# A two-layer diffusion backbone on one core: scratch tiles of their own in the merge, the last six feed-forward blocks by token groups, and five products ahead of layer 1's second norm

## The chip, the cores and the metric

The kernel runs on one core of a Trainium2 chip. The metric is the device time of one execution in microseconds (us); the median of several runs counts. The core has five engines, each of which works through its own queue in order: TensorE (PE in the profile; its weight loads are listed apart as PEld), VectorE (DVE), ScalarE (ACT), GpSimd (POOL) and SyncE (SP), which here only issues DMAs. Engines wait for each other by semaphores. Matmuls read SBUF and write PSUM.

## The reference

A diffusion backbone of two layers with D = 1024, over 512 latent tokens and 256 context tokens, 768 together. Cut to what matters:

```python
for l in range(2):
    mod = silu(c) @ w_mod[l] + b_mod[l]          # and mod_c from c_ctx, for the context tokens
    sh1, sc1, g1, sh2, sc2, g2 = split(mod, 6)
    h = rms_norm(x, norm1[l]) * (1 + sc1) + sh1
    na_q, na_k, na_v, gq, gk, gv, ga, gb = split(h @ w_in[l])
    ya = neighbourhood_attention(na_q, na_k, na_v)      # 8 heads, window 8 x 16, plus context
    yb = grouped_query_attention(gq, gk, gv)            # 8 query heads, 2 key heads
    merged = sigmoid(ga) * (ya @ w_pa[l]) + sigmoid(gb) * (yb @ w_pb[l])
    x = x + g1 * (merged @ w_o[l])
    h2 = rms_norm(x, norm2[l]) * (1 + sc2) + sh2
    a, u = split(h2 @ w_ffn_in[l], 2)                   # 2816 columns each
    x = x + g2 * ((silu(a) * u) @ w_ffn_out[l])
return rms_norm(x, final_norm)
```

The context tokens go through the same steps in layer 0; in layer 1 only the latent tokens are carried past the projections.

## The kernel before

**Tiles.** Activations are stored with the 1024 features in 8 tiles of 128 partitions (index k or j) and tokens along the free dimension. A float32 product is made of three reduced-precision ones: both operands are split into a high part and what is left of it (the low part), and TensorE does high by high, high by low and low by high for each of the 8 feature blocks. So a product of one 128-row block of weights with a span of tokens is 24 matmuls, of 512, 384 or 256 columns. `weight()` (L353) loads a block of weights into the ring `wr` (4 tiles), has ScalarE copy the high part into the ring `wh` (3 tiles, L357) and GpSimd, or VectorE where `eng` says so, subtract it into `wl` (3 tiles, L359). `halves()` (L381) does the same for an activation: ScalarE the tile `hi`, GpSimd the tile `lo`. All loads go through SP's one queue in the order they are issued in.

**Order.** The program is written engine by engine by a scheduler that simulates the program's timeline and so sets the order on each queue, except where the code holds TensorE's order by hand (`manual_schedule`): in the attention, and at the start of each layer's feed-forward, where `part` or `whole` products are listed in a fixed order and the second norm is put in between by due times (`NORM`, in us of TensorE's work: first the sum over squares `st`, then the broadcast `rb`).

**Merge** (`merge`, L1390 and following). Two branches, `gb` with yb and then `ga` with ya. For each of 8 blocks j: a gate product `pj` (its result t, a tile `qt`), the projection `pp`, and the sum into `mb` or into `mh` and `ml`. In layer 0 the modulation of the later parts (28 columns blocks, n from 16 to 43) is done beside it: `mod_one` (L434) loads 128 rows of `wmodT` and does two products with a sum on VectorE, one for the latent row of conditions (L441) and one for the context's (L439), whose full-size output is thrown away into a tile `junk`. `junk` and the scratch of `conditions` (L419) are taken from the ring `wh`. `MODS` says how many of these are done at each j. What is left of the 28 is done in layer 0's output projection, one per j.

**Layer 0's output projection** (`out_proj`) goes over two halves of 384 tokens, 8 blocks of `wo` each; per block a residual on VectorE, a square on ScalarE and its sum `acc` on VectorE.

**Layer 0's feed-forward** (`ffn`). Blocks f of 128 hidden columns, 22 in all; the first two are plain products, the other 20 are done as `quad`, a scheme of seven products of half size on each side for two by two blocks, with scratch tiles `tt` (`TEMPS` of them). The output product takes blocks by chunks of 4, woven in between the quads; the last chunk is what is left (blocks 20 and 21) and is done for one token group after the other, (0, 512) and (512, 768), with residual, square and `acc`. After each group `following` stores x and does the next layer's first norm for it.

**Norm.** `rstd` (L473 to L497): `st` matmuls over `acc`, VectorE adds the epsilon (`rs`, L493), GpSimd takes the power, `rb` matmuls spread it over partitions. `modulate` then does, per feature block, `u` on VectorE (L526), `h` on ScalarE (L527) and `hl` on VectorE (L528).

**Layer change.** Layer 1's first products are for `gk`, `gv` and `gq` 0, on the 512 latent tokens first and on the context after.

**Layer 1's second norm.** In layer 1 the output projection goes over two groups of 256 tokens; the second group's norm is what `late` puts into the start of `ffn_plain`, whose products for the first group (`pf`) run ahead of it. `ffn_plain` takes blocks f in four chunks and gives `qt` 5 tiles.

Functions that the change touches:

## Time and profile before

| | us |
|---|---|
| runs | 2028.03, 2028.92, 2032.21 |
| median | 2028.92 |
| profiled execution: time | 2031.42 |
| profiled execution: span | 2029.6 |
| PE busy | 1954.4 (96%) |
| DVE busy | 1373.0 (68%) |
| ACT busy | 884.9 (44%) |
| POOL busy | 532.4 (26%) |

The span is cut into 40 slices in the page; in tenths of a slice, and with the granted clock of TensorE in tenths of full speed:

```profile
PE   7999999989999999999999979999999989999998
...
PEclk7899999989999999999999989999999989999999
```

A slice is 50.7 us. The slices with a 7 or an 8 are the prologue, layer 0's merge (from about 430), the layer change (1177 to 1222), layer 1's second norm (1641 to 1666) and the end. Attention of layer 0 lies before 430, its output projection at 580 to 650, its feed-forward from there to 1177; layer 1's attention and merge run to about 1600, its feed-forward from 1650 to 2010. TensorE's share is an average; what a change is worth is read in the stretch it changes.

### The profile page before, as it was taken

The page shows a single profiled execution, that of the slowest core. Times are in us where ns is not written, and L with a number is a line of the kernel's source. Part 1 is how long each engine was busy: PE and PEld are TensorE (multiplying, and loading weights), DVE is VectorE, ACT ScalarE, POOL GpSimd, SP SyncE. Part 2 cuts the span into 40 slices and gives each one's busy share as a digit, 9 for nine tenths or more (in the row PEclk, how much of TensorE's full clock was granted, in tenths as well). Part 3 has the DMA queues.
Part 4 walks back from the last instruction along what each step waited for, and adds up shares of the span by engine and source line. Part 5 has one row for each costly group of instructions (what it writes and reads, how often), then busy time and mean ns, then how long its engine had stood idle before and what let it go on. Part 6 is the DMA issues. An engine that isn't in the chain of part 4 may idle for free. (4 is left out here: it accounts for less than half of the span.)

```text
span 2029.6 us, 29667 instructions
## 1 busy us (share of the span) xinstructions
PE 1954.4 (96%) x11468; PEld 1767.9 (87%) x11468; DVE 1373.0 (68%) x2470; ACT 884.9 (44%) x1640; POOL 532.4 (26%) x273
## 2 busy tenths in 40 slices
PE   7999999989999999999999979999999989999998
PEld 6888999977899999999899868889988988888887
DVE  7577888766987999888857576888643563232326
ACT  4466666542235543333424245666543442222224
POOL 6522222234300000000000134332345124435444
PEclk7899999989999999999999989999999989999999
DMA  7211122134563134456321322112223632323233
GB/s 285 70 56 42 37 60 79 58 117 133 182 240 123 60 123 142 144 177 215 118 73 52 103 95 63 51 52 63 76 86 112 197 95 87 113 82 112 75 122 94
DMA packets 74364, 216.50 MB, mean 107 GB/s; under 512 B 8560, under 2 KB 12784, under 8 KB 74224
## 3 DMA queue, kind: packets, MB, share of 16 engines
q1 hardware_dynamic: 74224, 214.61, 33.0%
q8 instruction: 90, 1.47, 0.3%
q14 instruction: 50, 0.41, 0.1%
HBM read 202.52 MB, written 6.82 MB: 103 GB/s over the span
## 5 line engine op out<-in xcount | busy, mean ns | idle before, releaser
L359 POOL TENSOR_TENSOR wl<-wr,wh 128x1024 fp32r<-128x1024 f32 (+2 forms) x177 | 388.6, 2200 | 1159.7 <-ACT wh L357 1152.5
L357 ACT ACTIVATE wh<-wr 128x1024 fp32r<-128x1024 f32 (+2 forms) x253 | 231.7, 917 | 568.4 <-issue 188.8
L372 PE MATMUL pj<-h,wh 128*128 128x512 f32 (+1 forms) x720 | 265.3, 372 | 8.5 <-ACT wh L357 4.4
L372 PE MATMUL pj<-hl,wh 128*128 128x512 f32 (+1 forms) x720 | 257.4, 358 | 3.1 <-DVE hl L528 3.1
L372 PE MATMUL pj<-h,wl 128*128 128x512 f32 (+1 forms) x720 | 256.5, 357 | 0.6 <-POOL wl L359 0.5
L372 PE MATMUL po<-ph,wh 128*128 128x512 f32 (+1 forms) x560 | 192.6, 345 | 0.0
L372 PE MATMUL po<-pl,wh 128*128 128x512 f32 (+1 forms) x560 | 192.5, 345 | 0.0
L372 PE MATMUL po<-ph,wl 128*128 128x512 f32 (+1 forms) x560 | 191.3, 345 | 0.0
L1577 PE MATMUL qu<-r,w 128*128 128x384 f32 x960 | 177.3, 337 | 5.7 <-ACT tt L1584 3.1
L1444 DVE SCALAR_TENSOR_TENSOR x<-po,G,x 128x256 f32<-128x256 f32 (+3 forms) x176 | 101.2, 589 | 120.5 <-PE po L372 120.3
L1577 PEld LDWEIGHTS qu<-r,w 128*128 128x128 f32 x960 | 167.5, 189 | 9.4 <-ACT tt L1584 6.2
L372 PEld LDWEIGHTS pj<-h,wh 128*128 128x128 f32 x720 | 139.4, 194 | 25.1 <-ACT wh L357 4.9
L372 PEld LDWEIGHTS pj<-h,wl 128*128 128x128 f32 x720 | 138.9, 193 | 21.0 <-POOL wl L359 1.5
L372 PEld LDWEIGHTS pj<-hl,wh 128*128 128x128 f32 x720 | 139.8, 194 | 19.2 <-DVE hl L528 4.0
L372 PE MATMUL pf<-hl,wh 128*128 128x512 f32 (+1 forms) x384 | 144.0, 375 | 2.2 <-DVE hl L528 2.1
L372 PE MATMUL pf<-h,wh 128*128 128x512 f32 (+1 forms) x384 | 144.0, 375 | 0.9 <-ACT h L527 0.9
L372 PE MATMUL pf<-h,wl 128*128 128x512 f32 (+1 forms) x384 | 143.4, 373 | 0.0
L1004 ACT ACTIVATE pth<-tp 128x512 fp32r<-128x512 f32 x176 | 103.5, 595 | 67.5 <-PE tp L1054 37.5
L1005 DVE TENSOR_TENSOR ptl<-tp,pth 128x512 fp32r<-128x512 f32 x176 | 119.7, 685 | 14.9 <-ACT pth L1004 13.2
L1469 ACT ACTIVATE w<-wr 128x512 fp32r<-128x512 f32 x120 | 73.7, 628 | 103.3 <-PE qv L1577 22.1
L372 PEld LDWEIGHTS po<-pl,wh 128*128 128x128 f32 x560 | 105.6, 189 | 13.2
L372 PEld LDWEIGHTS po<-ph,wl 128*128 128x128 f32 x560 | 104.9, 188 | 13.7
(243 smaller groups left out, 4436.6 us busy)
## 6 DMA issues: line engine op xcount, KB each, us to landing
wr<-wmodT SPq DMA_DIRECT2D x91, 512.0 KB, 3.8
wr<-wfi SPq DMA_DIRECT2D x88, 512.0 KB, 3.5
wr<-win SPq DMA_DIRECT2D x68, 512.0 KB, 3.5
wr<-wo SPq DMA_DIRECT2D x32, 512.0 KB, 4.1
wr<-wfo SPq DMA_DIRECT2D x40, 256.0 KB, 2.7
wr<-wfo SPq DMA_DIRECT2D x24, 384.0 KB, 3.0
wr<-wp SPq DMA_DIRECT2D x32, 256.0 KB, 3.1
x<-x SPq DMA_DIRECT2D x16, 384.0 KB, 7.7
```

The lines of the kernel that those rows point to most:

```text
L357: nc.scalar.activation(hi, raw, AF.Copy)
L359: (eng or nc.gpsimd).tensor_tensor(lo, raw, hi[:].bitcast(F32), op=ALU.subtract)
L372: nc.tensor.matmul(ps[:, : b - a], u[:, c], v[k][:, a:b], start=(k == 0 and i == 0), stop=(k == nk - 1 and i == 2),)
L1004: nc.scalar.activation(hi, tp, AF.Copy)
L1005: nc.vector.tensor_tensor(lo, tp, hi[:].bitcast(F32), op=ALU.subtract)
L1444: self.nc.vector.scalar_tensor_tensor(x[j][:, f:u], ps[:, f - a : u - a], self.G[l][i][:, s, j : j + 1], x[j][:, f:u], op0=ALU.mult, op1=A ...
L1469: nc.scalar.activation(t[:, :n], src, AF.Copy)
L1577: nc.tensor.matmul(banks[bank], u[:, c], v, start=(first and k == 0 and i == 0), stop=(k == kn - 1 and i == 2), skip_group_check=True)
```

## The change

1. `conditions` makes one scratch tile `junk` in its own pool, used by the silu of both rows and by `mod_one`; nothing but weights is taken from the ring `wh` there.
2. `halves` does the low part on VectorE and not on GpSimd.
3. `MODS`, indexed by `j > 1` and no longer by `j % 2`, does no product of the modulation for the first branch's j = 0 and 1, then one per j; in the second branch one for j = 0 and 1, then two: 20 in the merge. The output projection does 8.
4. The feed-forward's `silu` and `c22` write into the tile that they read (`more`, `u3`), and `TEMPS` goes from 7 to 4.
5. The last chunk of layer 0's output product is 6 blocks (16 to 21), the four chunks before it are woven as they were; its weights are loaded per j (384 KB) for each of the two token groups, with the low part on VectorE.
6. `load` gives VectorE the low part of layer 1's products that are outside the attention's plan (the first three, and the merge's gates).
7. In layer 1's feed-forward the low parts of blocks f below 3 are done on VectorE; those of f = 0 and their high parts have a ring of their own (`we`, 4 tiles, with `qt` 4); five products of the first group stand ahead of the second group's (before, three); the due time of the norm's sum is 7.0 (before, 2.1).

The diff:

```diff
-CHUNK = 4
+CHUNK, LAST = 4, 6
...
-EARLY, TEMPS = 2, 7
+EARLY, TEMPS = 2, 4
...
-MODS = ((1, 1), (2, 2))
-NORM = ((3.0, 3.9), (2.1, 3.6))
+MODS = ((0, 1), (1, 2))
+NORM = ((3.0, 3.9), (7.0, 3.6))
...
-    def weight(self, src, cols, eng=None):
+    def weight(self, src, cols, eng=None, pool=None):
+
         nc = self.nc
         raw = self.raw(src, cols)
-        hi = self.wpool.tile([P, cols], F32R, tag="wh", name=self.name("wh"))
+        tile = lambda tag: (pool or self.wpool).tile([P, cols], F32R, tag="we" if pool else tag, name=self.name(tag))
+        hi = tile("wh")
         nc.scalar.activation(hi, raw, AF.Copy)
-        lo = self.wpool.tile([P, cols], F32R, tag="wl", name=self.name("wl"))
+        lo = tile("wl")
...
-        nc.gpsimd.tensor_tensor(lo[:, :n], src, hi[:, :n].bitcast(F32), op=ALU.subtract)
+        nc.vector.tensor_tensor(lo[:, :n], src, hi[:, :n].bitcast(F32), op=ALU.subtract)
...
         crow = pool.tile([P, 2, D], F32, name=self.name("crow"))
+        junk = pool.tile([P, D], F32, name=self.name("junk"))
...
-            self.silu(crow[:, s], self.wpool.tile([P, D], F32, tag="wh", name=self.name("junk")))
-        return crow
+            self.silu(crow[:, s], junk)
+        return crow, junk
...
-            junk = self.wpool.tile([P, D], F32, tag="wh", name=self.name("junk"))
...
-        return self.weight(self.d["win"][l, BLOCK[what, j]], D)
+        first = l == 1 and not self.flow
+        return self.weight(self.d["win"][l, BLOCK[what, j]], D, self.nc.vector if first else None)
...
-                for _ in range(MODS[br][j % 2]):
+                for _ in range(MODS[br][j > 1]):
...
-            ph, src = second.setdefault(f // CHUNK, ([], [])), raws[f][:, : 2 * nh]
+            ph, src = second.setdefault(min(f, FB - LAST) // CHUNK, ([], [])), raws[f][:, : 2 * nh]
...
-                if f % CHUNK == 1 and f > CHUNK:
+                if f % CHUNK == 1 and CHUNK < f < FB - CHUNK // 2:
...
-        chunk = (FB - 1) // CHUNK
-        c0, c = chunk * CHUNK, FB - chunk * CHUNK
+        chunk = (FB - LAST) // CHUNK
         for a, b in groups:
             acc = None
-            for j in range(0, KB, 4):
-                w = self.weight(d["wfo"][l, j : j + 4, :, c0 * P :], 4 * c * P)
-                for i in range(4):
...
+            for j in range(KB):
+                w = self.weight(d["wfo"][l, j, :, chunk * CHUNK * P :], LAST * P, nc.vector)
+                ps = self.ps("a", "po")[:, : b - a]
+                drain(self.steps(ps, w, second[chunk], a, b, LAST))
+                self.residual(l, 1, ps, x, j, a, b)
+                acc = self.square(x[j], a, b, pool, acc)
...
-                    weights[f, up] = self.weight(d["wfi"][l, 2 * f + up], D)
+                    weights[f, up] = self.weight(
+                        d["wfi"][l, 2 * f + up], D, nc.vector if f < 3 else None, pool if f == 0 else None)
...
-                first = 2
+                first = 3
...
+                    ahead = [(0, 0), (0, 1), (1, 0), (1, 1), (2, 0)]
                     for f, up, g in (
-                        (0, 0, 0), (0, 1, 0), (1, 0, 0), (0, 0, 1), (0, 1, 1), (1, 0, 1), (1, 1, 0), (1, 1, 1)):
+                        *((f, up, 0) for f, up in ahead), *((f, up, 1) for f, up in ahead), (2, 1, 0), (2, 1, 1)):
...
-                        own = dict(acc=2, sq=2, u=2, qt=5) if last else dict(ws=1, tt=TEMPS, ps=7)
+                        own = dict(acc=2, sq=2, u=2, qt=4, we=4) if last else dict(ws=1, tt=TEMPS, ps=7)
...
-        s = self.t.temp(self.nh)
-        nc.vector.tensor_tensor(s, ps, more, op=ALU.add)
-        nc.scalar.activation(part, s, AF.Tanh, scale=0.5)
-        nc.vector.scalar_tensor_tensor(part, part, 1.0, s, op0=ALU.add, op1=ALU.mult)
+        nc.vector.tensor_tensor(more, ps, more, op=ALU.add)
+        nc.scalar.activation(part, more, AF.Tanh, scale=0.5)
+        nc.vector.scalar_tensor_tensor(part, part, 1.0, more, op0=ALU.add, op1=ALU.mult)
...
-        self.u = self.t.temp(self.nh)
-        self.t.nc.vector.tensor_tensor(self.u, ps, u3, op=ALU.add)
+        self.u = u3
+        self.t.nc.vector.tensor_tensor(u3, ps, u3, op=ALU.add)
```

How the order moves at three places follows. A row is the line, the operation, the output and its inputs, and the size; a name ends in a number that tells two tiles of one name apart.

The first place is ScalarE's queue at the end of layer 0's attention. `hi` are the high halves of the attention's outputs `yb`, `ys` are the attention's last tiles, `junk` is the scratch of the silu, `wh` are high weights, `t` is the first gate. Before:

```order
L384 ACTIVATE hi_5073<-yb_5059 128x768
L1012 ACTIVATE ys_4955<-y_4950 64x256
L1012 ACTIVATE ys_4963<-y_4958 64x256
L429 ACTIVATE junk_4982<-crow_4980 128x1024
L429 ACTIVATE junk_4987<-crow_4980 128x1024
L357 ACTIVATE wh_4997<-wr_4995 128x1024
L357 ACTIVATE wh_5079<-wr_5077 128x512
L357 ACTIVATE wh_5119<-wr_5117 128x512
L1385 ACTIVATE t_4994<-pj_5001 128x512
```

After:

```order
L359 ACTIVATE wh_5113<-wr_5111 128x512
L1388 ACTIVATE gt_4857<-pj_4859 128x256
L1007 ACTIVATE pth_4922<-tp_4917 128x512
L386 ACTIVATE hi_5068<-yb_5056 128x768
L1015 ACTIVATE ys_4937<-y_4926 64x256
L1007 ACTIVATE pth_4946<-tp_4941 128x512
L386 ACTIVATE hi_5072<-yb_5058 128x768
L1015 ACTIVATE ys_4955<-y_4950 64x256
L1015 ACTIVATE ys_4963<-y_4958 64x256
L432 ACTIVATE junk_4981<-crow_4980 128x1024 x2
L1388 ACTIVATE t_4993<-pj_5000 128x512
```

The first gate's high weight (`wh_4997`) stood behind the two `junk` before. It is `wh_4996` now, which stands 35 rows ahead of `wh_5113`, in the middle of the attention, with `wh_5078` between them; both silu stand where the weights stood.

The second place is VectorE's queue at the layer change. `acc` is the sum of squares of the first token group, `x` with 128x256 the residuals of the second group, `rs` the first group's mean square, `u` and `hl` layer 1's first norm, `wl` with 128x768 low weights of the last chunk. Before:

```order
L473 TENSOR_TENSOR acc_11677<-acc_11677,sq_11759 128x512
L1444 SCALAR_TENSOR_TENSOR x_6250<-po_11858,G_1_111,x_6250 128x256
L1444 SCALAR_TENSOR_TENSOR x_6252<-po_11869,G_1_111,x_6252 128x256
L1444 SCALAR_TENSOR_TENSOR x_6254<-po_11886,G_1_111,x_6254 128x256
L1444 SCALAR_TENSOR_TENSOR x_6256<-po_11897,G_1_111,x_6256 128x256
L1444 SCALAR_TENSOR_TENSOR x_6258<-po_11908,G_1_111,x_6258 128x256
L493 TENSOR_SCALAR rs_11775<-st_11770 128x4
L1444 SCALAR_TENSOR_TENSOR x_6260<-po_11919,G_1_111,x_6260 128x256
L526 SCALAR_TENSOR_TENSOR u_11785<-x_6246,A_0_108,rb_11778 128x512
L528 SCALAR_TENSOR_TENSOR hl_11784<-u_11785,mod_105,h_11783 128x512
```

After:

```order
L475 TENSOR_TENSOR acc_11308<-acc_11308,sq_11510 128x512
L1447 SCALAR_TENSOR_TENSOR x_6205<-po_11588,G_1_111,x_6205 128x256
L361 TENSOR_TENSOR wl_11672<-wr_11668,wh_11670 128x768
L1447 SCALAR_TENSOR_TENSOR x_6207<-po_11616,G_1_111,x_6207 128x256
L361 TENSOR_TENSOR wl_11701<-wr_11697,wh_11699 128x768
L495 TENSOR_SCALAR rs_11526<-st_11521 128x4
L1447 SCALAR_TENSOR_TENSOR x_6209<-po_11645,G_1_111,x_6209 128x256
L361 TENSOR_TENSOR wl_11730<-wr_11726,wh_11728 128x768
L1447 SCALAR_TENSOR_TENSOR x_6211<-po_11674,G_1_111,x_6211 128x256
L361 TENSOR_TENSOR wl_11759<-wr_11755,wh_11757 128x768
L528 SCALAR_TENSOR_TENSOR u_11536<-x_6205,A_0_108,rb_11529 128x512
L1447 SCALAR_TENSOR_TENSOR x_6213<-po_11703,G_1_111,x_6213 128x256
```

Seven of the eight residuals of the second group stood ahead of `rs` before; now two do, and the norm's `u` comes when half of the group's residuals are still to be done, with low weights in between. On TensorE the sum `st` stood 4 matmuls ahead of the second group's end and the broadcast right behind it; now they stand 41 and 76 matmuls into the group's 144.

The third place is TensorE's queue at layer 1's second norm: `pf` are products of the feed-forward, `st` the sum over squares, `rb` the broadcast. Before:

```order
L372 MATMUL pf_16851<-h_16547,wh_16846 128x256
L372 MATMUL pf_16851<-hl_16548,wh_16846 128x256
L372 MATMUL pf_16851<-h_16547,wl_16848 128x256
L484 MATMUL st_16873<-ones,acc_16591 128x1 x2
L372 MATMUL pf_16851<-h_16553,wh_16846 128x256
L372 MATMUL pf_16851<-hl_16554,wh_16846 128x256
L372 MATMUL pf_16851<-h_16553,wl_16848 128x256
L372 MATMUL pf_16889<-h_16511,wh_16883 128x256
```

After:

```order
L374 MATMUL pf_16804<-hl_16425,wh_16799 128x256
L374 MATMUL pf_16804<-h_16424,wl_16801 128x256
L486 MATMUL st_16823<-ones,acc_16474 128x1 x2
L374 MATMUL pf_16804<-h_16430,wh_16799 128x256
L374 MATMUL pf_16804<-hl_16431,wh_16799 128x256
L374 MATMUL pf_16804<-h_16430,wl_16801 128x256
L499 MATMUL rb_16832<-ident_sb,rs_16829 128x128 x2
L374 MATMUL pf_16804<-h_16436,wh_16799 128x256
```

Before, `st` stands in the first product of the first group, after its 21st matmul, and `rb` 15 matmuls later. Now it stands in the third product, after 66 matmuls, and `rb` 3 matmuls later.

More of the change, by code (lines that the diff above doesn't have):

```diff
@@ L431, in silu, with mod_one @@
         nc.vector.tensor_scalar(c, t, 0.5, None, op0=ALU.mult)
-    def mod_one(self, l, n, crow):
+    def mod_one(self, l, n, crow, junk):
         nc, d = self.nc, self.d
```

8 lines of the change are left out of this document (2 added, 6 removed).

## The prediction

> **What bounds the kernel now.** I read the page's shares first, then the busy time by stretch of time, then what TensorE waited for in the poor stretches, then single instructions there.
>
> ```profile
> PE 1954.4 (96%) x11468; PEld 1767.9 (87%) x11468; DVE 1373.0 (68%) x2470; ACT 884.9 (44%) x1640; POOL 532.4 (26%) x273
> ...
> core 0: 2029.6 us, clock 0.977
> ```
>
> TensorE is busy 96% of the span, so only its holes can be won or lost, plus the slow matmuls behind them. The stretches show where these lie; the columns are length, then busy time of PE, weight load, DVE, ACT and POOL, granted clock, DMA share and GB/s.
>
> ```profile
> 425.00:450.00 25.00, 19.78 (x98) 16.48 (x97) 16.09 (x22) 11.21 (x20) 13.55 (x7) 0.80 0.34 105
> 478.00:495.00 17.00, 12.94 (x54) 10.24 (x53) 10.72 (x14) 3.15 (x4) 11.22 (x6) 0.80 0.42 140
> 580.00:613.00 33.00, 31.53 (x183) 30.82 (x183) 25.02 (x39) 11.38 (x17) 0.00 (x0) 1.00 0.80 276
> 900.00:1010.00 110.00, 104.53 (x592) 98.04 (x591) 95.75 (x168) 38.27 (x70) 0.00 (x0) 1.00 0.54 172
> 1177.50:1222.00 44.50, 33.17 (x155) 27.80 (x154) 26.30 (x52) 18.33 (x35) 12.44 (x7) 0.77 0.16 48
> 1204.30:1222.00 17.70, 11.42 (x61) 10.19 (x62) 9.46 (x21) 7.43 (x16) 6.33 (x4) 0.61 0.09 30
> 1641.50:1666.00 24.50, 16.63 (x104) 15.35 (x103) 16.83 (x35) 9.89 (x24) 5.59 (x3) 0.79 0.17 56
> 1666.00:2010.00 344.00, 344.00 (x1631) 289.81 (x1631) 108.12 (x105) 98.47 (x131) 159.44 (x72) 1.00 0.31 97
> ```
>
> The row of 1666 to 2010 is the healthy case: busy all the time, clock 1.00. I call lost time the length less busy time times clock, since it takes in both the hole and the slow matmuls after it. The start of layer 0's merge loses 25 - 19.78 x 0.80 = 9.2 us, its change of branch 17 - 12.94 x 0.80 = 6.6, the layer change 44.5 - 33.17 x 0.77 = 19.0 (of which 17.7 - 11.42 x 0.61 = 10.7 from 1204 on, the second token group's norm, so 8.2 before it), layer 1's second norm 24.5 - 16.63 x 0.79 = 11.4. These four are 46 us, about what there is to win. What TensorE waited for in them, in total, times and the longest (the first two rows are the merge, the next three the layer change, the last the second norm):
>
> ```profile
> PE pj L372 <- ACT wh L357: 4.4, 2, 3.7
> PE pp L372 <- ACT wh L357: 2.8, 1, 2.8
> ...
> PE rb L497 <- POOL rs L494: 3.7, 2, 2.0
> PE pj L372 <- DVE hl L528: 3.1, 2, 2.0
> ...
> PE st L484 <- DVE acc L473: 1.8, 1, 1.8
> ...
> PE st L484 <- DVE acc L473: 4.8, 1, 4.8
> ```
>
> **Layer 0's merge.** At its start ScalarE makes the two scratch tiles of the conditions' silu out of the ring of high weights, and only behind them the first gate's weight:
>
> ```profile
> 432.15 1.99 ACT L429 ACTIVATE junk<-crow 128x1024 f32<-128x1024 f32 x2
> 434.05 1.80 ACT L357 ACTIVATE wh<-wr 128x1024 fp32r<-128x1024 f32 x2
> ...
> 435.14 0.80 PE L372 MATMUL pj<-h,wh 128*128 128x512 f32 x1 [3.67 <-ACT wh L357]
> ```
>
> TensorE stood 3.67 us. With a scratch tile of its own the ring isn't held, and in the new order two high weights and the first of the merge stand on ScalarE before the attention's last tiles. So the 3.67 goes, and of the slow matmuls after it (19.78 x 0.20 = 4.0 us) I take a third, since the attention's own last waits stay: 5.0, ends 3 and 8. Late next is the high tile of the last attention output.
>
> At the change of branch the same ring is held by a product of the modulation, which itself stood behind a weight of GpSimd:
>
> ```profile
> 482.65 2.90 POOL L359 TENSOR_TENSOR wl<-wr,wh 128x1024 fp32r<-128x1024 f32 x1 [1.96 <-ACT wh L357]
> ...
> 483.25 3.38 DVE L439 CUSTOM_DVE_ANT_0 junk<-wr,crow 128x1024 f32<-128x1024 f32 x1
> ...
> 486.67 0.63 ACT L357 ACTIVATE wh<-wr 128x512 fp32r<-128x512 f32 x1 [4.10 <-DVE mod L439]
> ...
> 487.39 0.47 PE L372 MATMUL pp<-hi,wh 128*128 128x512 f32 x1 [2.76 <-ACT wh L357]
> ```
>
> The high weight started when the product ended (486.6), and TensorE 2.76 us late. The tile of its own takes that link out, the first two blocks of this branch carry one product of the modulation and not two, and in the new order a gate's 21 matmuls stand ahead of the first use of the low halves. I take 2.8 plus most of the slow matmuls (12.94 x 0.20 = 2.6): 5.0, ends 2 and 6.6.
>
> Against it: 8 low halves go from GpSimd (1.83 us) to VectorE. The nearest rows are a 512 and a 1024 wide subtraction there:
>
> ```profile
> L359 DVE TENSOR_TENSOR wl<-wr,wh 128x1024 fp32r<-128x1024 f32 x36 | 43.9, 1222 | 11.0 <-ACT wh L357 10.7
> ...
> L359 DVE TENSOR_TENSOR wl<-wr,wh 128x512 fp32r<-128x512 f32 x40 | 27.5, 687 | 1.2
> ...
> L385 POOL TENSOR_TENSOR lo<-yb,hi 128x768 fp32r<-128x768 f32 x4 | 7.3, 1832 | 30.2 <-ACT hi L384 30.1
> ```
>
> Halfway between 0.69 and 1.22 is 0.95 us at 768 columns: 3.8 us for four halves, beside 21 matmuls of some 0.2 = 4.2 us. They fit, with 0.4 to spare. That they may not run at that price is shown by two tiles of VectorE beside GpSimd's weights:
>
> ```profile
> 1637.19 2.41 POOL L359 TENSOR_TENSOR wl<-wr,wh 128x1024 fp32r<-128x1024 f32 x1 [12.72 <-ACT wh L357]
> ...
> 1637.48 2.39 DVE L528 SCALAR_TENSOR_TENSOR hl<-u,mod,h 128x256 fp32r<-128x256 f32 x1 [0.87 <-ACT h L527]
> ...
> 1640.84 0.48 DVE L528 SCALAR_TENSOR_TENSOR hl<-u,mod,h 128x256 fp32r<-128x256 f32 x1 [0.18 <-ACT h L527]
> ```
>
> The same instruction took 2.39 us beside it and 0.48 without, and ended 0.27 after GpSimd did: 1.9 us is what one collision costs. The Trainium skill, page "SBUF — State Buffer", section "Who interferes with whom", says that a VectorE instruction with two inputs in SBUF and a GpSimd instruction that reads SBUF share a port pair, and that whichever starts first has it for its whole length. The rows agree. By that rule each moved half can be held as long as a weight of GpSimd lasts, so it speaks against this part of the change, and for the parts that take weights from GpSimd; it is a rival below.
>
> **Layer 0's output projection.** Merge now does 20 products of the modulation (none for j up to 1 and one after it, then one and two: 6 + 14), not 24, so 8 and not 4 fall here: 4 x 2 instructions of 1.22 = 9.8 us on VectorE and 2 MB more on the queue of SP.
>
> ```profile
> 591.46 1.23 DVE L439 CUSTOM_DVE_ANT_0 junk<-wr,crow 128x1024 f32<-128x1024 f32 x1 [3.78 <-PE po L372]
> ...
> x<-x SPq DMA_DIRECT2D x8, 384.0 KB, 8.1
> ...
> wr<-wmodT SPq DMA_DIRECT2D x2, 512.0 KB, 5.9
> ```
>
> VectorE is busy 25.0 of 33 us there (row of 580), so 8 of the 9.8 fit; the 3.78 us of waiting for a place in the ring goes as well. The loads queue behind x (8.1 us to landing), and VectorE works in order, so a product that waits for its row of weights holds the next low weight. In the new order the low weights of j 3 and 4 stand ahead of the first such product. I take -1.5 us (9.8 - 8, rounded down), ends -6 (half of the 9.8 is exposed and a landing besides) and +1 (the wait in the ring).
>
> **Layer 0's feed-forward.** 7 scratch tiles become 4, but the sums are written in place, so a quad takes 3 where it took 6. Gone is a writer; the reader that frees a tile is the same operation of VectorE. The ring of high weights has no junk in it, and the queue loads 16 x 384 KB for the last six blocks where it loaded 4 x 512 KB for two and 8 x 256 KB for four: 2 MB more. The 900 to 1010 row has VectorE at 95.75 of 110 us, so there is cover of 13%. I take 0, ends -5 and +5 (the 5.5 us lost in that row, either way).
>
> **The layer change.** Before, the first group's norm stood bare. The last chunk is 6 blocks and not 2, so the second group lasts 8 x 18 matmuls and covers it.
>
> ```profile
> 1183.02 0.75 DVE L526 SCALAR_TENSOR_TENSOR u<-x,A,rb 128x512 f32<-128x512 f32 x1 [2.94 <-PE rb L497]
> ...
> 1189.27 0.39 PE L372 MATMUL pj<-hl,wh 128*128 128x512 f32 x1
> 1189.49 0.39 PE L372 MATMUL pj<-h,wl 128*128 128x512 f32 x1
> ...
> L1444 DVE SCALAR_TENSOR_TENSOR x<-po,G,x 128x256 f32<-128x256 f32 x88 | 41.1, 478 | 16.8 <-PE po L372 16.7
> ```
>
> Two 512 wide matmuls start 0.22 us apart, so a 256 wide one takes some 0.12, and the second group 144 x 0.12 = 17.3 us. The sum over squares stands 41 matmuls into it (4.8 us), when the last square is long added; the broadcast 35 later (9.4), past the power of 0.7 to 1.0 us. VectorE's queue from there is the new limit: 8 low weights of 768 (8 x 0.95 = 7.6), 3 of 1024 (3.7), 8 residuals of 0.48 (3.8), 16 modulations of 0.75 (12): 27.1 us, and with about 5 until it has the sums, the last half is ready at 32. TensorE takes the three first products of layer 1 block by block, 9 x 0.23 = 2.0 us a block after 18.1, and wants the last at 18.1 + 7 x 2.04 = 32.4. It just holds. So of the 8.2 before 1204 I take 6.5 and 1 us off for the start of the last chunk, whose weights of 384 KB come through ScalarE and VectorE one by one: 5.5, ends 2 and 9. The second group's norm is as bare as before (10.7): its sum waits for everything above.
>
> **Layer 1's merge** has its lower weights on VectorE: 0.5, ends 0 and 1 (it lost little).
>
> **Layer 1's second norm.** The place of the sum moves from after 21 matmuls of 256 to after 66, from 2.5 to 7.9 us into the products. VectorE gets five or six low weights of 1.22 that were GpSimd's.
>
> ```profile
> 1641.89 2.39 POOL L359 TENSOR_TENSOR wl<-wr,wh 128x1024 fp32r<-128x1024 f32 x1 [2.30 <-ACT wh L357]
> ...
> 1642.30 2.27 DVE L528 SCALAR_TENSOR_TENSOR hl<-u,mod,h 128x256 fp32r<-128x256 f32 x1 [0.58 <-ACT h L527]
> ...
> 1648.64 3.60 DVE L473 TENSOR_TENSOR acc<-acc,sq 128x256 f32<-128x256 f32 x7
> ...
> 1652.39 0.98 PE L484 MATMUL st<-ones,acc 128*128 128x1 f32 x4 [4.77 <-DVE acc L473]
> ```
>
> Before, seven squares stood behind eight modulations, of which two were held by GpSimd (2.39, quoted above, and 2.27 against 0.48); the squares ended at 1652.2 and TensorE stood 4.77 us. After, the two holds fall away (3.7) and some 4 low weights come in (4.9), so the squares end about 1.2 us later, at 1653.4, and the last half of the first group, half as late, at 1649.1. The first product ends with it (1649.4), and 42 matmuls of 0.12 bring TensorE to the sum at 1654.4. The wait goes. The broadcast now stands only 3 matmuls behind the sum, so it waits some 0.65 us for the power; group 0's products then last until about 1662.5, and the second group's halves come until 1665, which leaves 2.5 bare. With the slow matmuls after both I count 6.8 of the 11.4 as still lost: 4.6, ends 1 and 8.
>
> **Sum:** 5.0 + 5.0 - 1.5 + 0 + 5.5 + 0.5 + 4.6 = 19.1 us. The profiled execution took 2031.42 (span 2029.6), 2.5 over the median of the runs, 2028.92; taken from the median it gives 2010.
>
> **The rivals.**
> - Half of it comes: VectorE, which receives about 40 us of work (some 16 low halves and 30 low weights), is the bound where the count left no room (the 0.4 us at the branch, the 32 against 32.4 at the layer change). The terms fall to 2 + 3 - 4 + 4 + 4.5: 2019. For it: those two margins. Against: only four places carry the work.
> - The port in the merge: each of the four halves at the branch is held 1.6 us by a weight of GpSimd, and the gain there is 5 - 6.4: 2016 to 2017. For it: the 3.38 us product above. Against: the halves stand in a group, and one weight of GpSimd holds only the first.
> - More comes: no weight of GpSimd near the modulations, a free ring of high weights in the feed-forward (+5), the upper ends of the merge: 2001.
> - Slower: the four scratch tiles of the feed-forward. ScalarE's copies work in order, so one that waits for VectorE to free a tile holds the weights behind it, and the next quad of TensorE. At 1.3 us a quad, 20 quads lose 26: 2036. It decides from 1.2 us a quad (19.1 + 4.1 over 20). For it: VectorE at 87% there. Against: half as many tiles are taken.
>
> **How the numbers follow.** The forecast has 0.50, half 0.20, the port 0.08, more 0.12, slower 0.10. The range 2000 to 2024 holds all but the slower case and the tails. A change under 0.2% (4.1 us) can't be told from none: faster than that is 0.86 (all but the slower case and a fifth of the half one), within it 0.04, slower 0.10.
>
> **What would show it.** In the profile after: no scratch tile of the conditions ahead of the merge's first weight, and no wait of 3.67 or 2.76 there; the wait of the sum on the squares gone from both norms save the layer change's second group; TensorE busy through the first group's norm. The prediction is wrong if the quads' cadence changes, if low weights of VectorE appear as what TensorE waits for, or if the layer change's second group loses much more or less than 10.7.

## The result, and the profile after

The changed kernel takes 2013.49 us (median of four runs, 2012.04 to 2016.31) where the kernel before takes 2029.05: the ratio is 0.9922, with a 95% interval of 0.9905 to 0.994. The forecast was 2010, in a range of 2000 to 2024. The profiled execution's span fell from 2029.6 to 2011.8, so by the traces 17.8 us are gone, by the medians 15.6.

The shares and the stretches of the profile after, with the same columns as before:

```profile
PE 1947.7 (97%) x11516; PEld 1767.4 (88%) x11516; DVE 1382.1 (69%) x2498; ACT 889.5 (44%) x1646; POOL 450.0 (22%) x236
```

```profile
425.00:450.00 25.00, 23.29 (x145) 20.54 (x145) 19.98 (x32) 11.90 (x24) 5.95 (x3) 1.00 0.28 94
478.00:495.00 17.00, 17.00 (x98) 14.99 (x97) 16.08 (x29) 4.23 (x7) 3.85 (x3) 1.00 0.46 156
568.00:585.00 17.00, 11.04 (x54) 10.26 (x53) 12.70 (x25) 4.12 (x7) 0.00 (x0) 0.90 0.74 257
645.00:684.00 39.00, 37.19 (x205) 35.91 (x204) 37.55 (x81) 22.71 (x53) 0.85 (x1) 0.96 0.20 66
1162.00:1193.00 31.00, 30.83 (x195) 27.65 (x193) 23.94 (x38) 14.59 (x24) 1.01 (x1) 1.00 0.44 133
1193.00:1211.00 18.00, 10.45 (x52) 9.22 (x53) 9.57 (x22) 8.34 (x17) 5.54 (x4) 0.62 0.09 30
1625.00:1650.00 25.00, 22.27 (x161) 20.86 (x160) 17.82 (x40) 10.68 (x25) 0.70 (x1) 0.93 0.29 100
```

Read as before (length less busy time times clock): the merge's start loses 1.7 us where it lost 9.2, its change of branch nothing where it lost 6.6. The layer change up to the second group's sum (1162 to 1193) loses 0.2, the second group's norm after it 18 - 10.45 x 0.62 = 11.5, much as before (10.7). Layer 1's second norm loses 4.3 in its 25 us where it lost 11.4 in 24.5. And one row is new: 568 to 585, the start of layer 0's output projection, loses 17 - 11.04 x 0.90 = 7.1, where the same place of the program (581 to 598 before) lost 1.4.

To compare kernels I cut each trace at the same places of the program: the last matmul of layer 0's attention, the first of the output projection, of the feed-forward, of the quads, the last of the quads, layer 1's first scores, its first feed-forward product and its first output chunk. Lost time in this table is a stage's length less its matmuls at the spacing that they have when nothing holds them (0.227, 0.173 and 0.118 us for 512, 384 and 256 columns, 0.11 for narrower ones), from the profiled execution of each. It gives a little more than the reading above, since it counts every slow matmul. Stages in which the kernels don't differ show how far two traces scatter: the quads lost 13.5 to 18.1 us, the attention of layer 1 with its merge 12.2 to 14.2. A trace is of one execution: those of e5_mods_front and e12_last2 are 4.8 and 3.4 us above the median of their kernel's runs and that of e7_norm_alone 3.4 under it, so for these three the table and the median can be that far apart.

| kernel | merge, layer 0 | output projection | start of feed-forward | layer change | layer 1's second norm | span |
|---|---|---|---|---|---|---|
| before | 18.2 | 2.2 | 2.0 | 21.5 | 12.9 | 2029.6 |
| after | 3.1 | 8.4 | 4.6 | 14.0 | 7.0 | 2011.8 |
| e1_merge | 3.1 | 7.6 | 3.6 | 22.2 | 11.8 | 2023.2 |
| e2_rows_free | 6.7 | 0.2 | 3.4 | 14.9 | 7.0 | 2010.3 |
| e3_taper | 2.9 | 0.2 | 14.7 | 15.0 | 7.1 | 2014.1 |
| e4_halves_pool | 6.3 | 6.7 | 4.3 | 14.8 | 7.0 | 2013.5 |
| e5_mods_front | 24.5 | 0.2 | 3.6 | 14.5 | 7.0 | 2026.2 |
| e6_lc_wl | 2.9 | 7.5 | 3.6 | 15.2 | 7.0 | 2013.4 |
| e7_norm_alone | 16.0 | 2.2 | 2.0 | 19.1 | 7.0 | 2017.1 |
| e8_ring | 10.5 | 2.7 | 6.6 | 13.7 | 7.0 | 2012.2 |
| e9_early_sum | 2.8 | 8.1 | 2.0 | 5.0 | 7.1 | 2003.1 |
| e10_norm_early | 4.3 | 9.0 | 3.5 | 14.6 | 10.1 | 2013.8 |
| e11_wl_pool | 2.7 | 6.2 | 4.4 | 14.9 | 9.8 | 2012.2 |
| e12_last2 | 4.1 | 8.9 | 3.7 | 23.8 | 6.9 | 2021.1 |

From before to after the merge gained 15.1, the layer change 7.5 and layer 1's second norm 5.9; the output projection lost 6.2 of it and the start of the feed-forward 2.6. That is 19.7 where the span fell by 17.8; the rest is scatter, and 0.4 us for the block f = 2 of layer 1's feed-forward, which is now done in two halves.

### The profile page after: what moved, and what is told of

Same layout as the page of the kernel before. It is cut to its first block, busy times and chain, and to the rows that moved or that the text cites. A ratio compares the mean times of both kernels' runs of the same rounds, so it can differ in the third digit from the quotient of the medians.

```text
span 2011.8 us, 29695 instructions
## 1 busy us (share of the span) xinstructions
PE 1947.7 (97%) x11516; PEld 1767.4 (88%) x11516; DVE 1382.1 (69%) x2498; ACT 889.5 (44%) x1646; POOL 450.0 (22%) x236
## 5 line engine op out<-in xcount | busy, mean ns | idle before, releaser
L361 POOL TENSOR_TENSOR wl<-wr,wh 128x1024 fp32r<-128x1024 f32 (+2 forms) x156 | 330.7, 2124 | 713.7 <-ACT wh L359 684.4
L1447 DVE SCALAR_TENSOR_TENSOR x<-po,G,x 128x256 f32<-128x256 f32 (+3 forms) x160 | 91.9, 588 | 113.3 <-PE po L374 113.0
L496 POOL TENSOR_TENSOR rs<-rs,expo 128x2 f32<-128x2 f32 (+2 forms) x8 | 6.2, 772 | 678.6 <-DVE rs L495 678.6
L374 PEld LDWEIGHTS pj<-hl,wh 128*128 128x128 f32 x720 | 137.7, 191 | 18.1 <-DVE hl L530 4.0
L1008 DVE TENSOR_TENSOR ptl<-tp,pth 128x512 fp32r<-128x512 f32 x176 | 119.8, 685 | 14.2 <-ACT pth L1007 12.5
L374 PEld LDWEIGHTS po<-ph,wh 128*128 128x128 f32 x560 | 105.7, 189 | 14.1 <-ACT wh L359 1.1
```

The lines of the kernel that those rows point to most:

```text
L361: (eng or nc.gpsimd).tensor_tensor(lo, raw, hi[:].bitcast(F32), op=ALU.subtract)
L374: nc.tensor.matmul(ps[:, : b - a], u[:, c], v[k][:, a:b], start=(k == 0 and i == 0), stop=(k == nk - 1 and i == 2),)
L496: nc.gpsimd.tensor_tensor(r[:, :nb], r[:, :nb], self.expo[:, :nb], op=ALU.pow)
L1008: nc.vector.tensor_tensor(lo, tp, hi[:].bitcast(F32), op=ALU.subtract)
L1447: self.nc.vector.scalar_tensor_tensor(x[j][:, f:u], ps[:, f - a : u - a], self.G[l][i][:, s, j : j + 1], x[j][:, f:u], op0=ALU.mult, op1=A ...
```

## Where the output projection's time went: rows of the modulation

TensorE's waits between 568 and 585 of the changed kernel, and VectorE there, with what ended the idle time ahead of an instruction:

```profile
PE po L374 <- ACT mh L1441: 3.3, 1, 3.3
PE po L374 <- DVE wl L361: 2.6, 1, 2.6
```

```profile
565.24 1.23 DVE L441 CUSTOM_DVE_ANT_0 junk<-wr,crow 128x1024 f32<-128x1024 f32 x1 [2.46 <-DMA wr<-wmodT]
...
571.52 1.22 DVE L441 CUSTOM_DVE_ANT_0 junk<-wr,crow 128x1024 f32<-128x1024 f32 x1 [0.59 <-DMA wr<-wmodT]
...
577.65 1.23 DVE L441 CUSTOM_DVE_ANT_0 junk<-wr,crow 128x1024 f32<-128x1024 f32 x1 [1.89 <-DMA wr<-wmodT]
...
578.80 0.68 DVE L1440 TENSOR_TENSOR t<-t,mb 128x512 f32<-128x512 f32 x1
```

VectorE is idle here and yet late. It works in order, and a product of the modulation at its head waits for its row of `wmodT`; behind it stand the sums of the merge's last block, which TensorE's output projection wants as `mh`. Two theories: the rows come late (they share the four tiles of the ring `wr` with the weights), or VectorE has too much to do whatever it waits for.

**The merge's part alone**, on the kernel before (with the feed-forward's sums written in place as in the change, which makes the room for the new tile):

```diff
-MODS = ((1, 1), (2, 2))
+MODS = ((0, 1), (1, 2))
...
+        junk = pool.tile([P, D], F32, name=self.name("junk"))
...
-        nc.gpsimd.tensor_tensor(lo[:, :n], src, hi[:, :n].bitcast(F32), op=ALU.subtract)
+        nc.vector.tensor_tensor(lo[:, :n], src, hi[:, :n].bitcast(F32), op=ALU.subtract)
...
-EARLY, TEMPS = 2, 7
+EARLY, TEMPS = 2, 4
```

> The kernel before with the merge's part alone (scratch tile of its own, low halves on VectorE, 20 products of the modulation in the merge) and the scratch tiles of the feed-forward written in place, without which the new tile has no room. If the merge's part does by itself what the trace of the changed kernel shows, the output projection starts some 13 us earlier than before (568 against 581.7), its first half then takes about 48 us where it took 41.6, and 7 us are left at its end; the later stages give nothing back: 2021 to 2023. If the loss in the output projection comes from a later part of the change, about 13 us stay: 2016.

It ran in 2024.68 us, 0.997 of before (0.9958 to 0.9982). The row of the table is that of the changed kernel as far as the feed-forward: 3.1 in the merge and 7.6 in the output projection. So the loss belongs to the merge's own part. The median is 2 us above what was expected; the span, 6.4 under before, agrees with it.

**The rows taken away**, the products kept:

```diff
-        w = self.raw(d["wmodT"][l * 48 + n])
+        held = l == 0 and 22 <= n < 36
+        w = crow[:, 1] if held else self.raw(d["wmodT"][l * 48 + n])
...
-            w, w, crow[:, 0], 1.0, 0.0, ALU.mult, ALU.add, self.mod[l][:, 0, n : n + 1])
+            junk if held else w, w, crow[:, 0], 1.0, 0.0, ALU.mult, ALU.add, self.mod[l][:, 0, n : n + 1])
```

> The changed kernel, in which the 14 products of the modulation in the merge's second branch read a tile that is there already, and no row of weights is loaded for them; so those modulations aren't the right ones. Theory of the rows: VectorE, which works in order, waits at the end of the merge for rows that come late through the ring of four (2.46, 0.59 and 1.89 us in the trace), and TensorE waits for the merge's last tiles behind it (3.3 and 2.6). Then both waits of TensorE go and the output projection's first half falls from 48.4 us to about 42: 2007. Theory of the work: VectorE has too much to do there whatever it waits for, since every instruction is still done; then 46 to 48 us stay and the time is within 2 us of 2013.

The output projection loses 0.2 and not 8.4, and its busy time has no hole:

```profile
572.00:640.00 68.00, 68.00 (x400) 68.00 (x400) 56.12 (x95) 33.00 (x49) 0.85 (x1) 1.00 0.61 209
```

VectorE did every one of the 14 products, so the loss there came from the rows. But the total came to 2010.51, 3.5 above what was expected: the merge now loses 6.7 and not 3.1, 2.6 of it in a wait of a gate product for `mb`. With no rows to wait for, VectorE's queue is ordered in another way, and a part of the gain went into a new wait: the two stages together lose 6.9 where they lost 11.5, so what the rows cost in all is 4.6 us and not 8.2.

**Fewer products at the end of the merge:**

```diff
-                for _ in range(MODS[br][j > 1]):
+                for _ in range(MODS[br][j > 1] if br == 0 or j < 6 else 0):
```

> The changed kernel with no product of the modulation beside the last two blocks of the merge (16 in the merge and 12 in the output projection, not 20 and 8). Theory of the rows: nothing on VectorE stands ahead of the last blocks' sums that waits for a load, so the wait of 3.3 us goes, and the output projection gets more rows in its second half; first half about 43 us, 2008 to 2010. Theory of the work: the four products only move a little further, the loss with them: 2012 to 2014.

The output projection is whole again (0.2), as the theory of the rows had it, and yet the time is 2015.79, no better than after (0.9931, 0.9915 to 0.9948). The loss moved on with the products, as the theory of the work had it, and by more than it gave (2012 to 2014): it is in the next stage, 14.7 where it was 4.6. There the second half's sum waits for VectorE, which now does four more products while it also makes the first half's norm:

```profile
625.00:655.00 30.00, 20.49 (x102) 19.37 (x101) 23.93 (x47) 14.33 (x27) 1.82 (x1) 0.82 0.32 105
```

```profile
PE st L486 <- DVE acc L475: 7.8, 1, 7.8
```

So rows are late at the end of the merge, and VectorE itself is short after it (in the 10 us up to the end of that sum it is idle for 0.83 us alone, in a wait for a row).

**More products early**, 24 in the merge:

```diff
-MODS = ((0, 1), (1, 2))
+MODS = ((1, 2), (2, 1))
```

> The changed kernel with the products of the modulation earlier: 1 and then 2 per block in the first branch, 2 and then 1 in the second, so 24 in the merge (as before) and 4 in the output projection. VectorE is busy 78 to 83% of the time in the merge's stretches and 97% of it after the output projection, so the work belongs into the merge, but early, where a row that comes late holds nothing that TensorE needs soon. If that is so, the output projection's loss of 8.4 us falls to 2 or 3 and nothing comes back in the feed-forward (4.6 or less): 2006 to 2008. If the end of the merge stays late since four rows still stand among the loads of the output projection's weights, 6 us or more stay lost: 2012 to 2014.

2023.21 us (0.9964, 0.9951 to 0.9977): the theory that early places are free fell. The output projection loses 0.2, but the merge 24.5. TensorE's waits there, and what ScalarE and SP's queue waited for between 455 and 505:

```profile
PE pp L374 <- ACT wh L359: 5.0, 4, 2.4
PE pp L374 <- POOL wl L361: 4.0, 4, 1.3
PE pp L374 <- DVE lo L387: 3.5, 1, 3.5
```

```profile
ACT wh L359 <- DMA wr<-wp: 20.8, 4, 6.9
```

```profile
SPq L350 <- DVE mod L443: 23.6, 9, 5.2
```

SP's queue waits for a product of the modulation to give back a place in the ring, the merge's own weights `wp` are loaded behind it, and TensorE gets them late. That wait alone isn't the cause: in the changed kernel SP's queue waits longer for the same products (30.2 us in 8 waits between 455 and 505), and TensorE isn't held. What differs is VectorE, which is full in this kernel:

```profile
455.00:483.00 28.00, 19.69 (x106) 16.03 (x105) 27.73 (x49) 3.99 (x6) 7.58 (x4) 1.00 0.56 188
```

Two products and the sums take VectorE some 7 us a block (four instructions of 1.22 us, of which one mostly takes 2.3 beside a weight of GpSimd, and 1.0 us of sums), and the loads of `wp` come 7 us apart; in the changed kernel, with one product, they come some 4.2 us apart, and TensorE is busy for all of the 21 us from 450 to 471. So the first branch's blocks have room for one product: with two VectorE is late, and through the ring of four the weights are. Placed too late, the products hold up the merge's last sums.

**The scratch tile in the ring of high weights again:**

```diff
-            self.silu(crow[:, s], junk)
+            self.silu(crow[:, s], self.wpool.tile([P, D], F32, tag="wh", name=self.name("junk")))
...
+            junk = self.wpool.tile([P, D], F32, tag="wh", name=self.name("junk"))
             nc.vector.tensor_tensor_reduce(
```

> The changed kernel with the scratch tile taken from the ring of high weights again. If the ring is what cost the merge, the two holes come back: the stretch from the end of the attention to the output projection loses 12 to 18 us and not 3.1. Fewer products beside the first two blocks of the second branch may save the second hole; then it is 8 to 10. The output projection, which then starts later, loses less than 8.4 if it was the rows that were late: 2019 to 2023.

The hole at the merge's start comes back (TensorE waits 3.3 us for `wh`), a smaller one at 441 with it, and the merge loses 10.5: the ring is 7.4 of the 15.1 gained there. The output projection, which starts 7.8 us later, loses only 2.7 and the feed-forward's start 6.6, so what the own tile brings by the first quad is 19.8 - 16.1 = 3.7 us. The time, 2015.54, is under what was expected, and the runs can't tell it from 2013.49. From the end of the attention to the first quad the kernels lost: before 22.4, after 16.1.

**The low halves on GpSimd again:**

```diff
-        nc.vector.tensor_tensor(lo[:, :n], src, hi[:, :n].bitcast(F32), op=ALU.subtract)
+        nc.gpsimd.tensor_tensor(lo[:, :n], src, hi[:, :n].bitcast(F32), op=ALU.subtract)
```

> The changed kernel with the low halves of the merge back on GpSimd. If VectorE is the better place, as counted (0.95 us against 1.83), the change of branch loses again: four halves are 7.3 us against a cover of 4.2, some 3 us in layer 0 and less in layer 1: 2016 to 2018. If the two collide on VectorE (the rival of the prediction), it loses nothing or gains: 2011 to 2013.

The merge loses 6.3 and not 3.1, as counted, but the output projection 6.7 and not 8.4: 2015.49 against 2013.49 (0.993, 0.991 to 0.995), which the runs can't tell apart. A gate product waits 3.0 us for `mb`. In the changed kernel the four halves at the change of branch took 0.95 us each: no weight of GpSimd ran between 477.2 and 487.0.

## The layer change

**The last chunk of two blocks again:**

```diff
-CHUNK, LAST = 4, 6
+CHUNK, LAST = 4, 2
...
-                if f % CHUNK == 1 and CHUNK < f < FB - CHUNK // 2:
+                if f % CHUNK == 1 and CHUNK < f < FB:
```

> The changed kernel with the last chunk of two blocks again, loaded per block, all else as changed. If the length of the second group is what covers the first group's norm, the stretch from the last quad to the second group's sum loses 8 to 10 us again and not 2.2, and the time is 2018 to 2020. If the order by itself (the norm's place in the queue) does it, it loses 4 or less.

2019.53 us (0.9968, 0.9954 to 0.9982), and the layer change loses 23.8, of which 11.6 ahead of the second group's sum (after: 2.2); some 1.5 of that is a wait for the last chunk's high weights. TensorE waits for the first group's norm as before:

```profile
PE pj L374 <- ACT h L529: 4.4, 1, 4.4
```

It is the length of the second group that covers that norm.

**One low weight from GpSimd to VectorE.** In the changed kernel the longest wait of the second group's norm is for the power, which stands behind a weight on GpSimd:

```profile
PE rb L499 <- POOL rs L496: 3.1, 1, 3.1
...
PE st L486 <- DVE acc L475: 0.4, 1, 0.4
```

```profile
1193.88 2.34 POOL L361 TENSOR_TENSOR wl<-wr,wh 128x1024 fp32r<-128x1024 f32 x1 [29.12 <-PE st L486]
1196.17 0.69 POOL L496 TENSOR_TENSOR rs<-rs,expo 128x2 f32<-128x2 f32 x1
```

```diff
-        first = l == 1 and not self.flow
+        first = l == 1 and (not self.flow or (what, j) == ("gq", 1))
```

> The changed kernel with one low weight, that of layer 1's second query block, on VectorE and not on GpSimd. In the trace it takes GpSimd 2.34 us and stands ahead of the power of the second group's norm at the layer change, and TensorE waits 3.1 us for that power. If the power's place is what costs, the stretch from that norm's sum to the first scores loses 9.3 to 9.8 us and not 11.8: 2011. If the loss is the chain of the norm itself, it stays at 11.5 or more.

The stage's total stayed (15.2), and the time too (2013.33). The wait only changed its name:

```profile
PE st L486 <- DVE acc L475: 2.7, 1, 2.7
...
PE rb L499 <- POOL rs L496: 1.1, 1, 1.1
```

The power's wait fell by 2.0 as it should, and the weight, now on VectorE, stood ahead of the last sum over squares: that wait rose by 2.3. The stretch after the sum alone lost 10.7 and not 11.8, the one ahead of it 4.5 and not 2.2.

**The second group's sum ahead.** That sum stood behind all of the first group's modulations on VectorE's queue. This kernel makes it on TensorE, from squares in tiles that are free by then, and starts the modulation later in the feed-forward:

```diff
-            free = 0.0
+            free = -4.0
...
+                if a < S:
+                    acc = self.square(x[j], a, b, pool, acc)
+                    continue
+                if j == 0:
+                    trio = pool.tile([P, T], F32, tag="ps", name=self.name("sq"))
+                if j < 3:
+                    sq = trio[:, j * CTX : (j + 1) * CTX]
+                elif j < 7:
+                    sq = pool.tile([P, nh], F32, tag="tt", name=self.name("sq"))[:, :CTX]
+                else:
+                    sq = pool.tile([P, D // 2], F32, tag="ws", name=self.name("sq"))[:, :CTX]
+                acc = [*(acc or []), sq]
+                nc.scalar.activation(sq, x[j][:, a:b], AF.Square)
```

> The changed kernel with two more edits. At the layer change the second group's squares go into tiles that are free by then, and TensorE sums all eight itself (16 matmuls of one column) in place of seven sums on VectorE; so that group's sum, power and broadcast stand among the first products of layer 1. And the first product of the modulation in layer 0's feed-forward starts after 15 us of TensorE's work there, not at once. If the second group's norm is bare only because its sum stood behind the first group's modulations, the stretch from the sum to the first scores and what is ahead of it lose 14 us before and 5 to 7 now. If VectorE's queue is the limit whatever the order, its eight modulations come after the first group's and 11 us stay. At the feed-forward's start the two products stand ahead of the norm's tiles, 2.4 us; if that is what TensorE waits for, 4.6 us lost become 2 to 2.5. Both right: 2003 to 2004; neither: 2013.

2006.33 us, 0.9899 of before (0.9881 to 0.9918); the span is 2003.1, 8.7 under that of the changed kernel. It is the fastest kernel of this study, though its interval and that of the changed kernel (0.9905 to 0.994) just overlap. The layer change loses 5.0, the feed-forward's start 2.0; the 28 more matmul records of one column there cost 3 us of TensorE that the table doesn't count as lost. The 18 us around the second group's first products, which are those of 1193 to 1211 in the changed kernel (10.45 us busy at 0.62):

```profile
1184.00:1202.00 18.00, 17.51 (x112) 15.64 (x110) 12.69 (x23) 11.48 (x23) 6.38 (x3) 1.00 0.09 30
```

The sum's matmuls stand between 1171 and 1182, among the second group's last output products and the first products of layer 1, and on VectorE the second group's eight modulations follow the first group's at once:

```profile
1187.69 3.23 DVE L528 SCALAR_TENSOR_TENSOR u<-x,A,rb 128x256 f32<-128x256 f32 x8 [0.50 <-PE rb L499]
1190.82 3.26 DVE L530 SCALAR_TENSOR_TENSOR hl<-u,mod,h 128x256 fp32r<-128x256 f32 x8
```

## Layer 1's second norm

**This part alone**, on the kernel before (its edits as in the diff of the change: `NORM`, the products ahead, `weight`, the ring `we`):

> The kernel before with the part on layer 1's second norm alone (five products ahead, the due time 7.0, the first low weights on VectorE, the ring for block 0). If this part acts by itself, the stretch from the first feed-forward product to the first output chunk loses 7 us and not 12.9, all else as before: 2023 to 2024. If it needs the other parts, less than 2 us come.

The stage loses 7.0, as in the changed kernel, and the time is 2022.36 (0.9975, 0.9954 to 0.9997), about 1 us under what was expected. This part stands by itself.

**The sum's place taken back, and the low weights taken back**, one at a time, on the changed kernel:

```diff
-NORM = ((3.0, 3.9), (7.0, 3.6))
+NORM = ((3.0, 3.9), (2.1, 3.6))
```

> The changed kernel with the due time of layer 1's second norm back at 2.1, so the sum stands after 21 matmuls of the first product and not after 66; five products stay ahead of the second group, and the low weights stay on VectorE. By the prediction's count the squares end at about the time that TensorE would reach the sum at the 66th; at the 21st it comes some 5 us too early and stands: the stretch loses 11 to 12 us and not 7.0. If the collisions with GpSimd's weights were what cost, it stays at 7 to 8.

```diff
-                        d["wfi"][l, 2 * f + up], D, nc.vector if f < 3 else None, pool if f == 0 else None)
+                        d["wfi"][l, 2 * f + up], D, None, pool if f == 0 else None)
```

> The changed kernel with the first six low weights of layer 1's feed-forward back on GpSimd, the place of the norm's sum as changed. If the collisions cost, some of the modulations take 1.5 to 2.4 us again and not 0.48, the squares end some 2 us later or earlier by what VectorE saves (4 x 1.2), and the stretch loses 9 to 11 us. If the place alone is what counts, VectorE is freer and it stays at 7 or falls.

The stage loses 10.1 with the early place and 9.8 with the weights on GpSimd, where the changed kernel loses 7.0 and the kernel before 12.9: 3.1 and 2.8 us, about half of the 5.9 each (11 to 12 were expected of the early place, so it cost less than counted). With the early place TensorE waits 4.8 us for the squares. With the weights on GpSimd the sum doesn't wait, and the first group's halves do:

```profile
PE st L486 <- DVE acc L475: 4.8, 1, 4.8
```

```profile
PE pf L374 <- DVE hl L530: 3.0, 2, 1.8
```

```profile
1626.94 0.48 DVE L530 SCALAR_TENSOR_TENSOR hl<-u,mod,h 128x256 fp32r<-128x256 f32 x1 [0.18 <-ACT h L529]
1628.39 2.17 DVE L530 SCALAR_TENSOR_TENSOR hl<-u,mod,h 128x256 fp32r<-128x256 f32 x1 [0.58 <-ACT h L529]
...
1631.53 1.53 DVE L530 SCALAR_TENSOR_TENSOR hl<-u,mod,h 128x256 fp32r<-128x256 f32 x1 [0.18 <-ACT h L529]
```

The first of these fences is of the kernel with the early place, the other two of the one with the weights on GpSimd; GpSimd's weights ran from 1627.94 to 1632.78 there. The times, 2016.40 and 2013.03, are too close to 2013.49 for these runs to tell.

## Why the prediction was right

The time lay in the range and the sign and size were right: 19.1 us were forecast, 15.6 came by the medians and 17.8 by the traces. The terms were less right than their sum. By the table three gains were counted 8.0 us too small together (the merge, the layer change, layer 1's second norm), and two losses 7.3 too small (the output projection, the feed-forward's start); that the errors cancel is luck. Point by point:

- **The merge: more than counted.** 5.0 + 5.0 were forecast; the two stretches gave 7.5 and 6.6, the whole stage 15.1. The step that was too small took "a third" of the slow matmuls at the start; with the hole gone the clock was 1.00 in both stretches and all of them went. Its cause was counted as the ring in the main. Taken back one at a time, the ring is 7.4 us of it (e8_ring) and the low halves on VectorE 3.2 (e4_halves_pool, which was counted as a risk and not as a gain); for the other 4.5 no run shows the cause, and the new places of the products are the candidate.
- **The output projection: the step that failed.** -1.5 was forecast with an end at -6; it is -6.2. The argument looked at the low weights of j 3 and 4 and found them ahead of the first product. What stood behind a product were the last sums of the merge itself, a few rows earlier in the same queue, and their rows came late through the ring (e2_rows_free). The sentence that a product that waits for its row holds what is behind it was right; it was applied one place too late. One of the signs that the prediction named for being wrong came true here: TensorE waited 2.6 us for a low weight of VectorE, which stood behind a product of the modulation.
- **The feed-forward: 0 was forecast.** The quads bear that out (16.4 and 16.8), so the rival of the four scratch tiles didn't happen, and a free ring of high weights gave nothing either. The start lost 2.6: two products of the modulation stand ahead of the norm's tiles on VectorE. Started later, the stage loses 2.0 as before (e9_early_sum).
- **The layer change: 5.5 was forecast, 7.5 came.** The last half of the first group was forecast for 32 us after that group's end and came after 32.2 (1157.4 to 1189.6); TensorE, which was to want it at 32.4, began its last block at 33.2 and didn't wait. The second group's norm was as bare as forecast (12.3 before, 11.8 after). That its sum has to wait for everything above was true of this order only.
- **Layer 1's merge: 0.5 was forecast.** The stage of which it is a part lost 14.0 and 12.6, within its scatter: not shown.
- **Layer 1's second norm: 4.6 was forecast, 5.9 - 0.4 came.** The squares ended 3.1 us ahead of TensorE (1638.6 against 1641.7), where 1.0 was counted; the broadcast waited 0.6, where 0.65 was. Both halves of the argument, place and collisions, are borne out by a run each.
- **The rivals.** "Half of it" named the right engine, VectorE, and the wrong places: the two margins it rested on held. The port in the merge didn't hold the halves, as GpSimd had no weight there at that time; the product of the modulation that started at 487.0, just after GpSimd's next weight, took 3.44 us where it takes 1.22. The rule of the Trainium skill, page "SBUF — State Buffer", section "Who interferes with whom", that a VectorE instruction with two inputs in SBUF contends with a GpSimd instruction that reads SBUF, agrees with the traces where a weight did run: 2.17 and 1.53 us against 0.48 in e11_wl_pool.

## What to carry to other kernels

In a queue that works in order, an instruction that waits for a load costs what stands behind it; before moving such instructions, list what follows them on their engine up to the next thing that the bottleneck needs, on both sides of the stage's border. Work that shares one small ring with the weights has no free place: where its engine has no room for it (two products a block here, 7 us of VectorE beside 4.2 of TensorE) it delays the weights, and later it delays the results. And a gain ahead of an engine that is nearly full comes back in part as waits further on, so count a change from one point where the engines are in step to the next, not by the hole that it closes.

## What the runs showed of the hardware

The seven sums over squares of the first group at the layer change fell from 1086 to 686 ns on average without any edit to them. The lines are of before and of after:

```profile
L473 DVE TENSOR_TENSOR acc<-acc,sq 128x512 f32<-128x512 f32 x7 | 7.6, 1086 | 0.0
```

```profile
L475 DVE TENSOR_TENSOR acc<-acc,sq 128x512 f32<-128x512 f32 x7 | 4.8, 686 | 0.1
```

The mean hides two kinds. Before, five of the seven took 0.67 or 0.68 us and two took 2.10 and 2.12, and these two started while GpSimd had a low weight; here is the first, with that weight ahead of it:

```profile
1167.94 2.56 POOL L359 TENSOR_TENSOR wl<-wr,wh 128x1024 fp32r<-128x1024 f32 x1 [3.15 <-ACT wh L357]
```

```profile
1168.96 2.10 DVE L473 TENSOR_TENSOR acc<-acc,sq 128x512 f32<-128x512 f32 x1
```

It ended 0.6 us after GpSimd did. After, these low weights run on VectorE, and GpSimd did nothing between 1125 and 1163, where the seven sums stand. This I had not counted.

A second thing: waits that are short in themselves leave TensorE slow for long. In the second group's norm at the layer change, with waits of 0.4, 3.1, 1.1, 2.0 and 1.1 us, the granted clock of an 18 us stretch was 0.62. It was 0.50 from 1194.8, which is 1.0 us into the wait of 3.1, to 1208.5, which is 3.6 us after the last wait ended; matmuls of 256 columns started 0.21 us apart until then and 0.12 after. With the waits gone (e9_early_sum) the clock was 1.00 at the same place of the program.
